# A two-layer hybrid decoder: the attention's values by seven block products, woven with queries, keys and memory keys, and fewer score steps

## The chip, the cores and the metric

The kernel runs on one core of a Trainium2 chip. A core has a matmul engine (PE, with its weight loads shown as PEld), a vector engine (DVE), a scalar engine (ACT), a general engine (POOL) and a queue engine (SP). Each runs its own instructions in order, and they wait for each other by semaphores. PE reads from the on-chip memory SBUF and writes to PSUM, which has eight banks of 128 x 512 floats. DMAs are issued from the queues of SP, ACT and POOL; only those issued from POOL can add to what they find at their destination.

The metric is the device time of one execution in microseconds (us), as the median of several runs. Everything is float32 at the input and the output.

## The reference

There are two decoder layers over 256 tokens of width 1024. Each layer is a half-step SwiGLU network, a token mixer, cross-attention into 256 memory tokens, and another half-step network. The change touches the mixer of layer 0, differential attention, and the memory keys of layer 0. Cut to what matters:

```python
def diff_attention(h, cos, sin, w_in, ..., subln, w_out, lambda_init):
    q, k, v = split(h @ w_in, 3)                 # 1024 columns each
    q = apply_rope(q, cos, sin) * (64 ** -0.5)   # 8 heads x 2 x 64; the factor is 0.125
    k = apply_rope(k, cos, sin)
    # v: 8 heads x 128
    s = einsum("bqhcd,bkhcd->bhcqk", q, k)       # two score matrices per head
    s = where(k_pos <= q_pos, s, -inf)
    p = softmax(s)
    a = p[:, :, 0] - lam * p[:, :, 1]
    o = einsum("bhqk,bkhe->bqhe", a, v)
    o = rmsnorm(o, subln) * (1.0 - lambda_init)
    return o @ w_out

def memory_cross_attention(h, mem, mem_norm, w_q, w_kv, w_o):
    k, v = split(rmsnorm(mem, mem_norm) @ w_kv, 2)   # 1024 columns each
    ...
```

## The kernel before

**Precision and granules.** Every large product is made of three matmuls (`mm3`, L262 to L264): each operand is split into a high part in the reduced format fp32r and a low part that is the rest, and high x high, high x low and low x high are summed in PSUM. A weight is loaded by SP into one of nine buffers of 1 MB (`wp`) and split in *granules* of 128 x 1024: ACT casts the high part (`whi`, L224), DVE subtracts for the low part (`wlo`, L225). Four buffers for each part (`hp`) limit how far the splits can run ahead of PE; the program asks for them two to three granules ahead (`ready`, `use`, `AHEAD`). A *host step* below is one granule used for both blocks of 128 tokens: twelve matmuls of 512 columns.

**Products.** `wide` multiplies all tokens by 512 columns: 8 row tiles x 2 token blocks x 3 = 48 matmuls. `stream` and `columns` make the same in steps that can be woven with others. `seven` makes a product of 2 x 2 blocks (token blocks x halves of the input width on one side, halves of the input width x two blocks of 512 columns on the other) from seven block products instead of eight. It needs sums of blocks: on the token side `combine` makes four (`mixes=True` in `Norm`; DVE sums, then ACT and DVE split them into `s_hi` and `s_lo`, L480 to L487), and on the weight side there are x1 = w11 + w12, x2 = x1 + w22, x4 = x2 + w21, x3 = w12 + w22. A weight sum (`Sum`, L187 and following) is made by DVE (L203) or by two accumulating DMAs of POOL (L199), each on one half of the tile. x2 and x4 are made in place on x1. A product step of `seven` takes one granule and makes six matmuls. Its products collect in two PSUM banks, and intermediate values are copied out in between. Both networks of each layer run `seven` for most gate and up columns; cross-attention runs it for its memory values.

**The order of work.** The builder keeps a planned clock (`Pipe`): each matmul group advances it, and follow-up work is registered with a due time (`pipe.after(us, f)`, the numbers in `T`), or with a due time and a condition (`pipe.when`). It is put into the program when the planned clock passes that time. Instructions then go to each engine in an order fixed when the kernel is built. `share` and `weave` interleave host steps with the fourteen product steps of a `seven`: the list of counts says how many host steps stand before each product.

**The attention stage** (`diff_attention`, about 189 to 313 us of the profile). Four `wide` calls make queries and keys of heads 0 to 3, then of heads 4 to 7. After each, `rope` rotates them (DVE, with an addition on POOL, L930), PE turns them (`qkt`, L939). After each key call four groups of `probs` follow, one for each head: ten short matmuls for two score matrices with their masks (`sc`, L970 to L974), then for both score matrices the maximum of each query block (L978, L979), the scaling by 0.125 (L980), the exponentials with their sums (ACT, L982, L984), the reciprocals, the factor lambda (L988), and the weighted difference (L990, L991). PE turns the result (`tp`, L997). Two `wide` calls make the values; `v_fin` scales them by the norm's factor (L1009). `heads` multiplies (`po`), normalises (`on`, L1030), turns (`otp`, L1035) and splits (`o_hi`, `o_lo`) for the output product. Between values and output stand half of the memory keys (`kv.k_units(kv.k_split, cs=(0,))`), which need the memory tokens fetched (`kv.fetch`, four DMAs on ACT's queue) and split (`kv.prep`, `mh` and `ml`). `out_b` is the output product in eight units of twelve matmuls; the input rows 4 to 7 of it are heads 4 to 7.

Of the kernel before, what the change touches and what calls it, by code (L numbers as in the profile page):

```python
# [15 lines left out]
P = 128  # L16
# [41 lines left out]
def trunk(ctx, tc, a, out):  # L58
# [302 lines left out]
    def seven(b1, b2, x, mix, after, order=(0, 1, 2, 3, 5, 4, 6), second="dma"):  # L361
# [3 lines left out]
        x1 = Sum(b11, b12)  # L365
# [60 lines left out]
    def out_b(src, nkt, lhs, fin, order, hooks={}):  # L426
# [18 lines left out]
        for half, k0 in [(c, k) for k in order for c in range(2)]:  # L445
            if (half, k0) in hooks:
                units.append(([], hooks[half, k0]))
            w = W(src, k0, 4, half * 512, 512)
            for k in range(k0, k0 + 4, 2):
                units.append(([Gran(k, 2, (w, 0, 512))], lambda *gr, half=half: run(*gr, half=half)))  # L450

# [447 lines left out]
    def diff_attention(norm, nxt, kv):  # L899
# [7 lines left out]
        def tables():  # L907
# [6 lines left out]
            tab["t"] = t  # L914

        def rope(ps, key):
# [4 lines left out]
            for t in range(2):  # L921
                c, s, n = (tab["t"][:, i + t, :] for i in (0, 2, 4))
# [10 lines left out]
            def turn():  # L933
# [9 lines left out]
                if key[0] == "k":  # L943
                    for i in range(4):
                        pipe.after(T["probs"][i], lambda i=i: probs(2 * key[1] + i // 2, i % 2))
            pipe.after(T["rot"], turn)

        def proj_fin(key):
            def fin(ps):
                if key == ("k", 1):  # L950
# [10 lines left out]
        def probs(c, j):  # L961
# [11 lines left out]
            for b in range(2):  # L973
                nc.tensor.matmul(sc[b].rearrange("p (i k) -> p i k", k=P)[:, 0:3:2, :], lhsT=id_bf, rhs=mask_bf,  # L974
                                 start=False, stop=True)
            for b in range(2):
                s = sc[b]
                nc.vector.tensor_reduce(st[:, 2 * b:2 * b + 1], s[:, 0:128], axis=AX.X, op=ALU.max, negate=True)  # L978
                nc.vector.tensor_reduce(st[:, 2 * b + 1:2 * b + 2], s[:, 128:384], axis=AX.X, op=ALU.max, negate=True)  # L979
                nc.vector.tensor_scalar(st[:, 4 + 2 * b:6 + 2 * b], st[:, 2 * b:2 * b + 2], 0.125, None, op0=ALU.mult)  # L980
                p = work("p", 384)
                nc.scalar.activation(p[:, 0:128], s[:, 0:128], AF.Exp, scale=0.125,  # L982
                                     bias=st[:, 4 + 2 * b:5 + 2 * b], accum_out=st[:, 8 + 2 * b:9 + 2 * b])
                nc.scalar.activation(p[:, 128:384], s[:, 128:384], AF.Exp, scale=0.125,  # L984
                                     bias=st[:, 5 + 2 * b:6 + 2 * b], accum_out=st[:, 9 + 2 * b:10 + 2 * b])
                ps.append(p)
            nc.vector.reciprocal(st[:, 12:16], st[:, 8:12])
            nc.vector.tensor_scalar(st[:, 14:16], st[:, 14:16], nlam, None, op0=ALU.mult)  # L988
            for qb, sl in ((0, slice(0, 128)), (1, slice(128, 384))):
                nc.vector.tensor_scalar(ps[0][:, sl], ps[0][:, sl], st[:, 12 + qb:13 + qb], None, op0=ALU.mult)  # L990
# [696 lines left out]
```

## Time and profile before

| | |
|---|---|
| median of 3 runs | 1257.79 us (1257.74 to 1258.11) |
| profiled execution, whole | 1258.38 us |
| its span, first to last instruction | 1256.6 us |
| granted PE clock | 0.999 |
| attention stage | about 189 to 313 us |
| weight DMAs of `da_w_in` from SP | 12 of 1 MB, median 5.2 us to land |
| accumulating DMAs of POOL | 72 of 512 KB |

The profile is of one execution. Its page gives, for each engine, the time in which it was busy; matmuls overlap in the pipeline, so that PE at 99% says that PE had always something under way, not that it ran at its peak. What PE costs is read from the distance between the starts of its matmuls. The list of waits says who stood still for whom. A wait that isn't in PE's list cost the kernel nothing, however long it was.

### The profile page before, as it was taken

How to read it: one execution, taken by the hardware profiler on the slowest of the kernel's cores; microseconds unless marked ns; L12 is line 12 of the kernel's file. 1: busy time of each engine (PE TensorE's matmuls, PEld its weight loads, DVE VectorE, ACT ScalarE, POOL GpSimd, SP SyncE). 2: the span in 40 equal slices, each digit the busy share in tenths (PEclk: the TensorE clock that was granted, in tenths of full speed). 3: DMA queues.
4: the chain of work that ended last, by engine and by line, in shares of the span. 5: the costliest groups of instructions: out<-in, count | busy, mean ns of one | idle time of the engine just before them, and what ended most of it. 6: DMA issues, size and time to landing. Idle time of an engine off the chain costs nothing.

```text
span 1256.6 us, 18186 instructions
## 1 busy us (share of the span) xinstructions
PE 1247.1 (99%) x6751; PEld 1071.7 (85%) x6751; DVE 1057.2 (84%) x1451; ACT 873.5 (70%) x1388; POOL 162.5 (13%) x139
## 2 busy tenths in 40 slices
PE   9999999999999999999999999999999999999997
PEld 7888888788998888888888889999998898888886
DVE  6998787887787999887998976798898887898886
ACT  6676764686676776767776756777876775877772
POOL 1101102101101111110111000022233100011100
PEclk9999999999999999999999999999999999999999
DMA  9989976445776688987879977665636586489961
GB/s 330 301 255 259 314 256 208 137 165 170 222 214 170 165 252 260 293 246 234 240 198 268 311 247 221 192 193 168 201 134 185 169 246 182 157 251 256 258 190 34
DMA packets 161195, 275.03 MB, mean 219 GB/s; under 512 B 7209, under 2 KB 43730, under 8 KB 161106
## 3 DMA queue, kind: packets, MB, share of 16 engines
q1 hardware_dynamic: 137744, 229.75, 53.4%
q0 software_dynamic: 19744, 38.28, 17.7%
q10 hardware_dynamic: 3618, 5.84, 1.4%
q8 instruction: 53, 0.87, 0.3%
q14 instruction: 36, 0.29, 0.1%
HBM read 271.72 MB, written 2.13 MB: 218 GB/s over the span
## 4 chain that ended last, share of the span: by engine, by line
PE 94%; DMA 2%; DVE 2%; ACT 2%; issue 1%; POOLq 0%; POOL 0%; SPq 0%; ACTq 0%; DVEq 0%
PE out L262 9%; PE out L264 9%; PE out L263 9%; PE seven L263 8%; PE seven L262 8%; PE seven L264 8%; PE htp L855 1%; PE up L263 1%; PE up L264 1%; PE up L262 1%; PE xs L264 1%; PE xs L262 1%; PE xq L263 1%; PE xq L264 1%; PE xs L263 1%; PE xq L262 1%
## 5 line engine op out<-in xcount | busy, mean ns | idle before, releaser
L225 DVE TENSOR_TENSOR wlo<-w,whi 128x1024 fp32r<-128x1024 f32 (+2 forms) x532 | 639.4, 1220 | 134.6 <-ACT whi L224 126.8
L224 ACT CAST whi<-w 128x1024 fp32r<-128x1024 f32 (+2 forms) x534 | 551.0, 1039 | 245.2 <-PE out L264 84.0
L262 PE MATMUL out<-whi,hid_hi 128*128 128x512 f32 x336 | 132.3, 394 | 0.0
L264 PE MATMUL out<-whi,hid_lo 128*128 128x512 f32 x336 | 131.0, 390 | 0.0
L263 PE MATMUL out<-wlo,hid_hi 128*128 128x512 f32 x336 | 130.8, 389 | 0.0
L263 PE MATMUL seven<-wlo,s_hi 128*128 128x512 f32 x272 | 106.0, 390 | 0.6 <-DVE wlo L225 0.6
L262 PE MATMUL seven<-whi,s_hi 128*128 128x512 f32 x272 | 106.2, 390 | 0.0
L264 PE MATMUL seven<-whi,s_lo 128*128 128x512 f32 x272 | 105.9, 389 | 0.0
L199 POOL DMA_DIRECT2D w<-in_ffn_w_up_dram x30 | 36.7, 1268 | 346.6 <-DVE wlo L225 339.5
L203 DVE TENSOR_TENSOR w<-w 128x2048 f32<-128x2048 f32 x32 | 73.2, 2287 | 2.0 <-DMA w<-in_ffn_w_gate_dram 1.5
L264 PEld LDWEIGHTS out<-whi,hid_lo 128*128 128x128 f32 x336 | 63.1, 188 | 13.4
L263 PEld LDWEIGHTS out<-wlo,hid_hi 128*128 128x128 f32 x336 | 63.1, 188 | 12.6
L262 PEld LDWEIGHTS out<-whi,hid_hi 128*128 128x128 f32 x336 | 63.1, 188 | 12.5
L262 PE MATMUL seven<-whi,xh 128*128 128x512 f32 x180 | 70.5, 392 | 0.0
L264 PE MATMUL seven<-whi,xl 128*128 128x512 f32 x180 | 70.1, 389 | 0.0
L263 PE MATMUL seven<-wlo,xh 128*128 128x512 f32 x180 | 70.0, 389 | 0.0
L263 PEld LDWEIGHTS seven<-wlo,s_hi 128*128 128x128 f32 x272 | 51.1, 188 | 11.4 <-DVE wlo L225 1.0
L264 PEld LDWEIGHTS seven<-whi,s_lo 128*128 128x128 f32 x272 | 51.1, 188 | 10.7
L262 PEld LDWEIGHTS seven<-whi,s_hi 128*128 128x128 f32 x272 | 51.1, 188 | 10.4
L199 POOL DMA_DIRECT2D w<-in_ffn_w_gate_dram x30 | 36.9, 1467 | 176.2 <-DVE xst L1146 62.3
L264 PEld LDWEIGHTS seven<-whi,xl 128*128 128x128 f32 x180 | 33.8, 188 | 7.1
L262 PEld LDWEIGHTS seven<-whi,xh 128*128 128x128 f32 x180 | 33.8, 188 | 6.8
(395 smaller groups left out, 3013.7 us busy)
## 6 DMA issues: line engine op xcount, KB each, us to landing
w<-in_ffn_w_up_dram SPq DMA_DIRECT2D x40, 1024.0 KB, 7.8
w<-in_ffn_w_down_dram SPq DMA_DIRECT2D x40, 1024.0 KB, 9.3
w<-in_ffn_w_gate_dram SPq DMA_DIRECT2D x38, 1024.0 KB, 8.9
w<-in_ssd_w_in_dram SPq DMA_DIRECT2D x24, 1024.0 KB, 5.4
w<-in_xa_w_kv_dram SPq DMA_DIRECT2D x16, 1024.0 KB, 6.4
w<-in_ffn_w_gate_dram POOLq DMA_DIRECT2D x30, 512.0 KB, 9.7
w<-in_ffn_w_up_dram POOLq DMA_DIRECT2D x30, 512.0 KB, 7.2
w<-in_da_w_in_dram SPq DMA_DIRECT2D x12, 1024.0 KB, 5.2
```

The costliest lines, as they stand in the source:

```text
L199: nc.gpsimd.dma_start(self.t[:, k:k + 2, :], w.src[r0:r0 + 2 * P, w.c0:w.c0 + w.n] .rearrange("(k p) c -> p k c", p=P), accum_op=ALU.add)
L203: nc.vector.tensor_tensor(self.t, self.l.t, w.t, op=ALU.add)
L224: nc.scalar.copy(hv, src)
L225: self.eng.tensor_tensor(self.lo[:, :, o:o + n], src, hv.bitcast(F32), op=ALU.subtract)
L262: nc.tensor.matmul(o, lhsT=lh, rhs=rh, start=start, stop=False, skip_group_check=onto)
L263: nc.tensor.matmul(o, lhsT=lh, rhs=rl, start=False, stop=False, skip_group_check=onto)
L264: nc.tensor.matmul(o, lhsT=ll, rhs=rh, start=False, stop=stop, skip_group_check=onto)
L855: nc.tensor.transpose(tp[:, j, t * P:(t + 1) * P], us[t][:, (i + j) * P:(i + j + 1) * P], ident)
```

## The change

It does five things, all in layer 0's attention.

1. The values come from one `seven` over both blocks of 512 columns (w11 from column 2560, w12 from column 2048) in place of two `wide` calls, with a new `v_fin` for the evictions. `Norm` for this stage now makes the token-side sums (`mixes=l == 0`). x1 is no longer a DVE sum of two loaded tiles: a new argument `first="dma"` loads a second copy of w11 and lets DMAs add w12 to it; x2 is added by DMA as well.
2. The fourteen product steps are woven with twenty host steps: queries and keys of heads 0 to 3, of heads 4 to 7, and the memory keys. The counts are 5, 3, 2, 2, 3, 2, 1; two host steps of memory keys are left for the end.
3. In `probs` one reduction of 384 columns gives three maxima (it was two reductions for each score matrix), and one tiny minimum joins the last two for both matrices. The factor 0.125 moves into a rotation table for the queries, and lambda goes into the second scalar of a scaling.
4. Due times: the second half's score groups come at 0.8 of their times, and their turning after 7.0 instead of 8.5.
5. `kv.fetch` and `kv.prep` come earlier, and the sixth and seventh of the eight output units change places, so that the rows of heads 6 and 7 are asked for last.

```diff
-    def seven(b1, b2, x, mix, after, order=(0, 1, 2, 3, 5, 4, 6), second="dma"):
+    def seven(b1, b2, x, mix, after, order=(0, 1, 2, 3, 5, 4, 6), second="dma", first=None):
...
-        x1 = Sum(b11, b12)
+        x1 = Sum(W(b1[0], 0, 4, b1[1], 512) if first else b11, b12, first)
         x2 = Sum(x1, b22, second)
...
+        if pairs:
+            units[-3], units[-2] = units[-2], units[-3]
...
-            tab["t"] = t
+            tq = slot("cossinq")[:, :192].rearrange("p (i f) -> p i f", f=32)
+            nc.vector.tensor_scalar(tq, t, 0.125, None, op0=ALU.mult)
+            tab.update(k=t, q=tq)
...
-                        pipe.after(T["probs"][i], lambda i=i: probs(2 * key[1] + i // 2, i % 2))
+                        pipe.after(T["probs"][i] * (0.8 if key[1] else 1.0), lambda i=i: probs(2 * key[1] + i // 2, i % 2))
...
-                if key == ("k", 1):
+                if key == ("k", 0):
                     kv.fetch()
...
+            top = st[:, 0:6].rearrange("p (b i) -> p b i", i=3)
             for b in range(2):
-                s = sc[b]
-                nc.vector.tensor_reduce(st[:, 2 * b:2 * b + 1], s[:, 0:128], axis=AX.X, op=ALU.max, negate=True)
-                nc.vector.tensor_reduce(st[:, 2 * b + 1:2 * b + 2], s[:, 128:384], axis=AX.X, op=ALU.max, negate=True)
-                nc.vector.tensor_scalar(st[:, 4 + 2 * b:6 + 2 * b], st[:, 2 * b:2 * b + 2], 0.125, None, op0=ALU.mult)
+                nc.vector.tensor_reduce(top[:, b, :], sc[b][:, 0:384].rearrange("p (i k) -> p i k", k=P), axis=AX.X,
+                                        op=ALU.max, negate=True)
+            nc.vector.tensor_tensor(top[:, :, 1], top[:, :, 1], top[:, :, 2], op=ALU.min)
+            for b in range(2):
                 p = work("p", 384)
-                nc.scalar.activation(p[:, 0:128], s[:, 0:128], AF.Exp, scale=0.125,
-                                     bias=st[:, 4 + 2 * b:5 + 2 * b], accum_out=st[:, 8 + 2 * b:9 + 2 * b])
-                nc.scalar.activation(p[:, 128:384], s[:, 128:384], AF.Exp, scale=0.125,
-                                     bias=st[:, 5 + 2 * b:6 + 2 * b], accum_out=st[:, 9 + 2 * b:10 + 2 * b])
+                for qb, sl in ((0, slice(0, 128)), (1, slice(128, 384))):
+                    o = 8 + 2 * b + qb
+                    nc.scalar.activation(p[:, sl], sc[b][:, sl], AF.Exp, bias=top[:, b, qb:qb + 1], accum_out=st[:, o:o + 1])
                 ps.append(p)
             nc.vector.reciprocal(st[:, 12:16], st[:, 8:12])
-            nc.vector.tensor_scalar(st[:, 14:16], st[:, 14:16], nlam, None, op0=ALU.mult)
...
-                nc.vector.tensor_scalar(ps[0][:, sl], ps[0][:, sl], st[:, 12 + qb:13 + qb], None, op0=ALU.mult)
-                nc.vector.scalar_tensor_tensor(ps[0][:, sl], ps[1][:, sl], st[:, 14 + qb:15 + qb], ps[0][:, sl],
+                nc.vector.tensor_scalar(ps[1][:, sl], ps[1][:, sl], st[:, 14 + qb:15 + qb], nlam, op0=ALU.mult, op1=ALU.mult)
+                nc.vector.scalar_tensor_tensor(ps[0][:, sl], ps[0][:, sl], st[:, 12 + qb:13 + qb], ps[1][:, sl],
                                                op0=ALU.mult, op1=ALU.add)
...
-            pipe.after(T["tp"], turn)
+            pipe.after(7.0 if c > 1 else T["tp"], turn)
...
+        def v_fin():
+            t, vs = {}, {}
+
+            def after(i, b):
+
+                def copy():
+                    t[i] = work(f"v{i}")
+                    nc.scalar.copy(t[i], b[i])
+
+                def put(r, n, x):
+                    vs[r, n] = slot("v")
+                    nc.scalar.activation(vs[r, n], x, AF.Copy, scale=norm.col[:, r:r + 1])
+                    if r:
+                        for c in (2 * n, 2 * n + 1):
+                            pipe.when(T["heads"] + 1.5 * (c - 2 * n), lambda c=c: {2 * c, 2 * c + 1} <= ats.keys(),
+                                      lambda c=c: heads(c, [vs[q, n] for q in range(2)]))
+
+                def c12():
+                    nc.vector.tensor_tensor(t[3], b[2], t[3], op=ALU.subtract)
+                    nc.scalar.copy(b[2], t[1])
+                    put(0, 0, t[3])
+
+                def c22():
+                    nc.vector.tensor_tensor(t[0], t[0], b[5], op=ALU.subtract)
+                    put(1, 0, t[0])
+                pipe.after(0.7, {0: copy, 1: copy, 3: copy, 2: c12, 5: c22, 4: lambda: put(0, 1, b[4]),
+                                 6: lambda: put(1, 1, b[6])}[i])
+                if i == 2:
                     kv.prep()
+            return after
...
-        for c in range(2):
-            wide([(w_in, c * 512, 512)], norm, "q", proj_fin(("q", c)))
-            wide([(w_in, 1024 + c * 512, 512)], norm, "k", proj_fin(("k", c)))
-        for c in range(2):
-            wide([(w_in, 2048 + c * 512, 512)], norm, "v", v_fin(2 * c))
-        kv.k_units(kv.k_split, cs=(0,))
-        out_b(a["da_w_out"][0], KT, ot, upd(1.0, nxt), (0, 4), {(0, 0): kv.fetch, (0, 4): kv.mix})
+            host += stream([(w_in, c * 512, 512)], norm, "q", proj_fin(("q", c)))
+            host += stream([(w_in, 1024 + c * 512, 512)], norm, "k", proj_fin(("k", c)))
+
+        def mk_fin(c):
+            def fin(ps):
+                kv.k[c] = ps
+                kv.k_split(c)
+            return fin
+        host += columns(a["xa_w_kv"][0], 0, kv, "mk", [mk_fin(0), mk_fin(1)])
+        weave(share(host, seven((w_in, 2560), (w_in, 2048), norm.x, norm.s, v_fin(), (1, 0, 3, 2, 5, 4, 6), "dma", "dma"),
+                    [5, 3, 2, 2, 3, 2, 1]))
+        out_b(a["da_w_out"][0], KT, ot, upd(1.0, nxt), (0, 4), {(0, 0): kv.fetch, (0, 4): kv.mix}, pairs=True)
...
-        nx = Norm(gains("mix_norm", l), first=l == 1)
+        nx = Norm(gains("mix_norm", l), first=l == 1, mixes=l == 0)
```

More of the change, by code (lines that the diff above doesn't have):

```diff
@@ L424, in down, with out_b @@
                 for k in range(w.k0, w.k0 + w.nk, 2)]
-    def out_b(src, nkt, lhs, fin, order, hooks={}):
+    def out_b(src, nkt, lhs, fin, order, hooks={}, pairs=False):
         banks = [[], []]
@@ L921, in rope @@
             for t in range(2):
-                c, s, n = (tab["t"][:, i + t, :] for i in (0, 2, 4))
+                c, s, n = (tab[key[0]][:, i + t, :] for i in (0, 2, 4))
                 x = ps[t].rearrange(r, x=2, f=32)
@@ L1000, in turn @@
                 ats[2 * c + j] = at
-            pipe.after(T["tp"], turn)
-        def v_fin(c0):
-            def fin(pv):
-                for c in range(c0, c0 + 2):
-                    v = v2(slot("v"))
-                    cs = slice((c - c0) * 256, (c - c0 + 1) * 256)
-                    for t in range(2):
-                        nc.scalar.activation(v[:, t, :], pv[t][:, cs], AF.Copy, scale=norm.col[:, t:t + 1])
-                    pipe.when(T["heads"] + 1.5 * (c - c0), lambda c=c: {2 * c, 2 * c + 1} <= ats.keys(), lambda c=c, v=v: heads(c, v))
-                if c0 == 0:
+            pipe.after(7.0 if c > 1 else T["tp"], turn)
[22 more added lines that the diff above has]
+                if i == 2:
                     kv.prep()
-            return fin
+            return after
         def heads(c, v):
@@ L1018, in heads @@
                 at = ats[2 * c + j]
-                vs = v[:, :, j * P:(j + 1) * P]
-                nc.tensor.matmul(po[:, j, 0, :], lhsT=at[:, 0:128], rhs=vs[:, 0, :], start=j == 0, stop=False)
-                nc.tensor.matmul(po[:, j, 1, :], lhsT=at[:, 128:256], rhs=vs[:, 0, :], start=False, stop=False)
-                nc.tensor.matmul(po[:, j, 1, :], lhsT=at[:, 256:384], rhs=vs[:, 1, :], start=False, stop=j == 1)
+                o = c % 2 * S + j * P
+                vs = [x[:, o:o + P] for x in v]
+                nc.tensor.matmul(po[:, j, 0, :], lhsT=at[:, 0:128], rhs=vs[0], start=j == 0, stop=False)
+                nc.tensor.matmul(po[:, j, 1, :], lhsT=at[:, 128:256], rhs=vs[0], start=False, stop=False)
+                nc.tensor.matmul(po[:, j, 1, :], lhsT=at[:, 256:384], rhs=vs[1], start=False, stop=j == 1)
             ss = sm.tile([P, 16], F32, name="ss", tag="ss")
@@ L1041, in heads @@
             pipe.after(T["otp"], turn)
+        host = []
         for c in range(2):
-            wide([(w_in, c * 512, 512)], norm, "q", proj_fin(("q", c)))
-            wide([(w_in, 1024 + c * 512, 512)], norm, "k", proj_fin(("k", c)))
-        for c in range(2):
-            wide([(w_in, 2048 + c * 512, 512)], norm, "v", v_fin(2 * c))
-        kv.k_units(kv.k_split, cs=(0,))
-        out_b(a["da_w_out"][0], KT, ot, upd(1.0, nxt), (0, 4), {(0, 0): kv.fetch, (0, 4): kv.mix})
+            host += stream([(w_in, c * 512, 512)], norm, "q", proj_fin(("q", c)))
[9 more added lines that the diff above has]
+        out_b(a["da_w_out"][0], KT, ot, upd(1.0, nxt), (0, 4), {(0, 0): kv.fetch, (0, 4): kv.mix}, pairs=True)
     def split2(src, name):
```

## The prediction

> **What bounds the kernel now.** I read the page's busy times and its chain of waits first, then the list of who waited for whom on the matmul engine.
>
> ```profile
> span 1256.6 us, 18186 instructions
> PE 1247.1 (99%) x6751; PEld 1071.7 (85%) x6751; DVE 1057.2 (84%) x1451; ACT 873.5 (70%) x1388; POOL 162.5 (13%) x139
> ...
> PE 94%; DMA 2%; DVE 2%; ACT 2%; issue 1%; POOLq 0%; POOL 0%; SPq 0%; ACTq 0%; DVEq 0%
> ```
> ```profile
> PE warm L597 <- DVE warm L99: 1.5, 1, 1.5
> PE seven L263 <- DVE wlo L225: 0.6, 1, 0.6
> PE acs L1285 <- PE mk L264: 0.2, 1, 0.2
> ```
>
> The chain that ended last is 94% PE, and the second fence is the whole list of PE's waits: 2.3 us in 1256.6, none of it in the attention stage. So the time is the number of matmuls times the pace at which they start. A matmul left out is paid in full; work added to another engine costs nothing until it makes PE wait, and then it is paid in full too.
>
> The next view gives busy times by stretch (us, then busy us of PE, PEld, DVE, ACT, POOL, then clock, DMA share, GB/s): the attention stage, its first half, the FFN that follows, and that FFN's densest 40 us.
>
> ```profile
> 190.00:313.00 123.00, 123.00 (x694) 102.08 (x694) 97.00 (x203) 80.16 (x195) 20.29 (x15) 1.00 0.52 171
> 190.00:256.00 66.00, 66.00 (x345) 52.49 (x344) 52.73 (x112) 37.31 (x81) 13.76 (x9) 1.00 0.54 187
> 410.00:540.00 130.00, 130.00 (x593) 107.92 (x593) 117.67 (x115) 94.60 (x111) 17.16 (x14) 1.00 0.83 238
> 420.00:460.00 40.00, 40.00 (x186) 33.27 (x185) 38.57 (x37) 29.50 (x36) 4.93 (x4) 1.00 0.79 227
> ```
>
> The clock is 1.00 throughout. DVE has 26.0 us free in the attention stage (123.00 less 97.00). The FFN, which already runs seven products for eight, keeps PE full with DVE busy for 90% of 130 us, and for 96% (38.57 of 40) in its densest part. That is the yardstick for what the stage will bear.
>
> **The matmuls.** The values are now two `wide` calls of 48 matmuls of 512 columns, 96 in all. `seven` makes 7 products x 4 k x 3 = 84. Twelve go. Their price stands in the FFN's timeline of PE, where one product starts exactly twelve matmuls after another:
>
> ```profile
> 441.08 0.39 PE L262 MATMUL seven<-whi,s_hi 128*128 128x512 f32 x1
> ...
> 443.80 0.39 PE L262 MATMUL seven<-whi,xh 128*128 128x512 f32 x1
> ```
>
> 443.80 - 441.08 = 2.72 us (0.227 each; the shown 0.39 overlaps its neighbours). Queries, keys, memory keys, scores, transposes and the output keep their number of matmuls: they only change places. **The whole gain is 2.72 us**, provided PE still never waits.
>
> **What DVE gets and loses.** Rows of the view that groups instructions by line and shape (xcount | busy us, mean ns of one | idle before):
>
> ```profile
> L225 DVE TENSOR_TENSOR wlo<-w,whi 128x1024 fp32r<-128x1024 f32 x36 | 45.6, 1278 | 13.2 <-ACT whi L224 13.2
> L979 DVE TENSOR_REDUCE st<-sc 128x1 f32<-128x256 f32 x16 | 6.6, 412 | 0.0
> L978 DVE TENSOR_REDUCE st<-sc 128x1 f32<-128x128 f32 x16 | 4.5, 279 | 2.4 <-PE sc L974 2.4
> L980 DVE TENSOR_SCALAR st<-st 128x2 f32<-128x2 f32 x16 | 2.5, 159 | 0.1
> L988 DVE TENSOR_SCALAR st<-st,lam 128x2 f32<-128x2 f32 x8 | 1.8, 223 | 0.1
> L459 DVE SCALAR_TENSOR_TENSOR ml<-my,cols,mh 128x256 fp32r<-128x256 f32 x8 | 3.5, 478 | 0.0
> ```
> ```profile
> L1140 DVE TENSOR_REDUCE xst<-xs 128x2 f32<-128x512 f32 x4 | 2.7, 682 | 0.0
> L486 DVE TENSOR_TENSOR s_lo<-sraw,s_hi 128x512 fp32r<-128x512 f32 x4 | 2.7, 683 | 0.0
> L837 DVE TENSOR_TENSOR p<-p,seven 128x512 f32<-128x512 f32 x4 | 2.7, 680 | 0.0
> L481 DVE TENSOR_TENSOR sraw<-y 128x256 f32<-128x256 f32 x4 | 1.5, 417 | 0.0
> ```
>
> - Seven products split 14 granules of weights where two `wide` calls split 8: 6 x 1.278 = +7.7.
> - `mixes=True`: eight block sums and four low parts, 8 x 0.417 + 4 x 0.683 = +6.1.
> - `c12` and `c22` (as L837): 2 x 0.68 = +1.4.
> - The scores lose 16 x (0.412 + 0.279 + 0.159) + 8 x 0.223 = 15.4 and get 16 reductions of 384 columns and eight tiny minima. The trace has no such reduction; it lies between 0.412 (256 columns) and 0.682 (512). I take the middle, 0.55: 8.8 + 8 x 0.16 = 10.1, net -5.3 (the ends of that bound: -7.5 to -3.2).
> - The query table, one instruction on 192 elements, lies between 0.16 (L980) and 0.417 (L481): taken as 0.3, near the smaller.
>
> Together +10.2: 107.2 of 120.3 us, 89%, under the FFN's 90%. On that average it is hidden. Uncovered it would cost what exceeds the room, which is the last rival.
>
> **ACT and POOL.**
>
> ```profile
> L224 ACT CAST whi<-w 128x1024 fp32r<-128x1024 f32 x91 | 95.4, 1052 | 38.7 <-PE out L264 16.2 <-PE seven L264 12.3 <-issue 2.7
> ...
> L547 ACT ACTIVATE y<-xt,cols 128x256 f32<-128x256 f32 x8 | 3.1, 480 | 0.0
> ...
> L833 ACT ACTIVATE p<-p,rcol 128x512 f32<-128x512 f32 x4 | 2.9, 721 | 0.0
> ```
>
> ACT gets 6 splits (6.3), 8 copies of y (3.8), and 12 instructions on 512 columns (four high parts, four copies, four value evictions) at 0.72 or less (8.7): 80.2 + 18.8 = 99.0 of 120.3 at most, before the eight old value evictions are taken off. Not a bound. SP's queue issues one more weight load (the second copy of w11); the DMA share of 0.52 leaves room.
>
> POOL gets the eight issues of four sums; L199's issues run 1.2 to 1.74 us:
>
> ```profile
> L199 POOL DMA_DIRECT2D w<-in_ffn_w_gate_dram x30: 1197/1533/1742, 48.8 to 1173.7; - x30
> ...
> DMA to landing us min/median/max: 5.7/7.4/13.8
> ```
>
> Three of the four sums have several products' time to land. **The tight one is x2**, built in place on x1 with only two host steps between the product that reads x1 and the one that reads x2. Cross-attention does this same chain now; POOL's and PE's timelines show its lead:
>
> ```profile
> 325.58 1.23 POOL L199 DMA_DIRECT2D w<-in_xa_w_kv_dram  x1 [5.45 <-DVE xsq L1127]
> 328.39 1.22 POOL L199 DMA_DIRECT2D w<-in_xa_w_kv_dram  x1 [1.58 <-DVE wlo L225]
> ```
> ```profile
> 331.19 0.40 PE L262 MATMUL seven<-whi,s_hi 128*128 128x512 f32 x1
> ```
>
> The halves of x2 go out 5.6 and 2.8 us before x1's product starts (331.19), as x1's granules are split. At the median 7.4 they land at +1.8 and +4.6. PE asks for x2 at +2.72 (the product) + 5.44 (two host steps of twelve matmuls) = +8.2 and, for the second half, at +9.5; whi and wlo take 1.05 + 1.28 of that. So 4.0 and 2.6 us are to spare: I cost it at nothing. Both at the longest landing, 13.8, would be 2.4 and 3.8 late. Behind a sum that waits on POOL stand the first keys' rotation additions and the next sums; behind x2's `wlo` on DVE stand the first score groups; and PE waits for both.
>
> The Trainium skill's page "DMA: Bandwidth & Descriptors", section "Anatomy of one DMA", puts such a transfer at 2 us plus its bytes at 436 GB/s, an estimate of 3.2 us for 512 KB. The quickest here took 5.7, so I go by the trace; by the page the sum would be the same with more to spare.
>
> **What moves.** The memory keys' 96 matmuls go ahead of the output, with `prep` and the fetch of the memory blocks (four DMA issues of ACT) ahead of them; the work is the same, and the same DMAs stood in ACT's queue before. `seven` holds two of the eight PSUM banks through the whole stage, which the old values did not: a score group that finds no free bank would wait, in the same place and for the same time as in the first rival below, where I count it. I cost the moves at nothing.
>
> **The end of the stage.** Fewer score steps shorten the chain maxima, exponentials, scaling, transposes, heads, output. But the planner now allows 7.0 us for the last four groups where it allowed 8.5, and the values end later relative to the output. The last group of before, by line (PE's and DVE's timelines):
>
> ```profile
> 265.48 0.49 PE L970 MATMUL sc<-qk 64*128 64x128 f32 x4
> ...
> 278.54 0.49 PE L997 MATMUL tp<-ident,p 128*128 128x128 f32 x3
> ```
> ```profile
> 276.38 0.74 DVE L991 SCALAR_TENSOR_TENSOR p<-p,st 128x128 f32<-128x128 f32 x2
> ```
>
> Its p was done at 277.12, 1.4 us before PE transposed it. Allowing 1.5 less while the group saves some 0.7 of DVE time (5.3 / 8) leaves about +0.6. I cost it at nothing, with little cover; the bounds are 0 and 1.5 us for each of four groups, and a first wait also lets DVE catch up, so that I count two of the four at most (3.0).
>
> **The sum.** 1256.6 - 2.72 = 1253.9 for the profiled span. The profiled execution took 1258.38, 1.8 more than its span, and lies 0.6 above the median of the timed runs, so on that median: 1257.79 - 2.72 = **1255.1 us**, 0.22% less. About 0.2% (2.5 us) is what a measurement of this kernel can tell from no change, so a wait of only 0.2 us already turns it from faster to the same.
>
> **The rivals.**
>
> *A late group of scores (0.25).* The 1.4 us of spare above speak for it, PE's empty list of waits against. One wait of 1.5: 1256.6; range 1255.4 to 1258.1.
>
> *x2 lands late (0.10).* With the longest landing, up to 3.8: 1258.9. Against it stands a DMA share of 0.52 here.
>
> *DVE becomes the bound between the first query step and the last key step, and the kernel is slower (0.13).* Sixteen host steps and ten product steps stand there now. PE's own time for them:
>
> ```profile
> 189.38 0.39 PE L262 MATMUL q<-whi,xh 128*128 128x512 f32 x1
> ```
> ```profile
> 242.09 0.39 PE L262 MATMUL v<-whi,xh 128*128 128x512 f32 x1
> ```
>
> From 189.38 to 242.09 sixteen host steps with their transposes and scores took 52.7; ten product steps of 1.36 make 66.3. DVE's row for 190 to 256 was 52.73. Into the same time come about 6.5 more granules (8.3), the mixes (6.1), c12 and c22 (1.4) and the memory's low parts (8 x 0.478 = 3.8), less four score groups' saving (2.6): 69.7, or 3.4 over, unless the fourth rotation and fifth score group, which fall after this point in the new order, take their share out again (the rotation is 2.6 by the two rows below, the group about as much: an estimate of 5): 64.7, 1.6 under.
>
> ```profile
> 243.35 0.68 DVE L925 TENSOR_TENSOR rt<-k,cossinr 128x512 f32<-128x512 f32 x1
> ...
> 245.54 0.41 DVE L929 TENSOR_TENSOR rt<-k,cossinr 128x256 f32<-128x256 f32 x1
> ```
>
> It decides against the change when DVE's need there passes 66.3 + 2.7 = 69.0. POOL could push it there: beside the rotation's addition on POOL a split took 2.00 us for 1.22,
>
> ```profile
> 202.73 2.00 DVE L225 TENSOR_TENSOR wlo<-w,whi 128x1024 fp32r<-128x1024 f32 x1
> ```
>
> and eight new POOL issues at 0.78 each are 6.2: 64.7 + 6.2 = 70.9, 4.6 over, 1259.7; with the 5 staying in, 1264.7. I give this rival the middle, 1262. The Trainium skill's page "SBUF — State Buffer", section "SBUF: two separate sides", says that a DVE instruction with two SBUF inputs and a GpSimd one that reads SBUF hold the shared ports as an exclusive lock; the 2.00 agrees. Against this rival: in the FFN's densest 40 us four such issues (4.93 us of POOL) ran with DVE at 96% and PE never waited.
>
> That the change doesn't do what it says is no rival for the matmuls, which are counted in the code; for the score steps it is: they lie off the chain, so their 5.3 us of DVE buy no time by themselves.
>
> **Chances.** Forecast, no wait over 0.3 us: 0.52, of it 0.46 faster by over 0.2%. With the rivals: faster 0.46, the same 0.43 (small waits and most of the first two rivals), slower 0.11. The likeliest case's own range is 1254.6 to 1255.4; the 8-in-10 range reaches through the first two rivals, 1254.6 to 1258.9.
>
> **What would show it.** Right: 12 fewer matmuls, PE's list of waits still about 2.3 us, DVE near 107 of some 120 us in the stage. First rival: PE waiting for p at L997's place, or for `on` or `o_lo`. Second: `wlo` of x2 waiting for a DMA, and PE behind it. Third: whi done early, wlo late, PE waiting for wlo in many places, splits beside POOL well over 1.22.

## The result and the profile after

The changed kernel takes 1265.61 us (median of 6 runs, 1264.07 to 1266.41), the kernel before 1257.93 (6 runs, 1257.74 to 1258.33) beside it. The ratio is 1.0059, with a 95% interval of 1.0046 to 1.0072: slower, where 1255.1 was forecast with a range up to 1258.9. The profiled execution took 1265.59, its span 1263.8. Lines of the changed file are shifted: score matmuls are L974 to L978, the rotation's addition L934, the copy of the turned queries and keys (`qk`) L945, the copy of the turned scores (`at`) L1002.

From the page after, the line of busy times and the one of the chain; then the four largest entries of the list of who PE waited for (total us, times, longest):

```profile
PE 1248.7 (99%) x6739; PEld 1071.4 (85%) x6739; DVE 1069.4 (85%) x1440; ACT 886.3 (70%) x1406; POOL 174.8 (14%) x147
...
PE 78%; DVE 2%; issue 0%; ACT 0%; POOL 0%; POOLq 0%
```
```profile
PE sc L974 <- ACT qk L945: 2.6, 1, 2.6
PE po L1043 <- ACT at L1002: 2.1, 2, 1.2
PE warm L599 <- DVE warm L99: 1.5, 1, 1.5
PE qkt L943 <- POOL rt L934: 0.9, 1, 0.9
```

Twelve matmuls fewer, as counted (6739 for 6751), and yet PE is busy 1.6 us longer. Three of the four are new, and all stand in attention. PE's timeline gives the stage's first matmul and the first one behind it, then the first one behind it in the kernel before:

```profile
189.06 0.39 PE L262 MATMUL q<-whi,xh 128*128 128x512 f32 x1
```
```profile
320.45 0.28 PE L262 MATMUL mk<-mh,whi 128*128 128x256 f32 x1
```
```profile
313.06 0.28 PE L262 MATMUL mk<-mh,whi 128*128 128x256 f32 x1
```

320.45 - 189.06 = 131.39 us; before it was 313.06 - 189.38 = 123.68. The difference, 7.71, is the whole loss (1265.61 - 1257.93 = 7.68). With the 2.72 that went, PE lost 10.4 us inside the stage. The windows (PE, PEld, DVE, ACT, POOL, granted clock, DMA share, GB/s) say where, and that waits are not all of it; the last row is the kernel before:

```profile
190.00:256.00 66.00, 62.41 (x306) 49.35 (x305) 57.71 (x106) 43.79 (x89) 13.66 (x11) 0.97 0.71 203
190.00:320.00 130.00, 124.31 (x679) 101.76 (x678) 109.49 (x189) 90.80 (x208) 25.70 (x19) 0.97 0.65 192
...
190.00:223.00 33.00, 32.12 (x152) 26.50 (x151) 31.55 (x50) 20.57 (x32) 8.71 (x8) 1.00 0.82 235
...
227.50:231.00 3.50, 3.47 (x14) 2.46 (x15) 2.13 (x4) 0.92 (x3) 1.20 (x1) 0.53 1.09 201
...
293.50:296.00 2.50, 2.50 (x9) 2.06 (x9) 2.50 (x5) 1.48 (x9) 0.43 (x1) 0.58 0.28 61
```
```profile
190.00:223.00 33.00, 33.00 (x164) 27.12 (x164) 23.35 (x38) 16.12 (x23) 7.65 (x5) 1.00 0.57 194
```

On the average of the stage DVE is at 109.49 of 130 us, 84%. In its first 33 us it is at 31.55, 96%, for 23.35 before. And right behind the long waits the clock is granted at 0.53 and 0.58. What that costs is seen by run 1 below, where the same matmuls run with the clock at 1.00: from the first score matmul behind the wait to the next product it is 3.26 us here (227.53 to 230.79) and 1.78 there, and from the `po` at 292.46 to the next transpose 3.64 here and 2.16 there. That is about 1.5 us each. With the waits (2.6 + 2.1 + 0.9) it makes 8.6 of the 10.4; for the rest the list has no entry over 0.2 in the stage.

**The largest wait, backwards.** ACT's timeline, then POOL's, DVE's and PE's:

```profile
225.00 1.99 ACT L224 CAST whi<-w 128x1024 fp32r<-128x1024 f32 x2 [4.35 <-DMA w<-in_da_w_in_dram]
226.90 1.06 ACT L945 COPY qk<-qkt 128x512 f32<-128x512 f32 x2
```
```profile
209.64 1.24 POOL L199 DMA_DIRECT2D w<-in_da_w_in_dram  x1 [14.59 <-DVE cossinr L915]
211.22 2.96 POOL L934 TENSOR_TENSOR rt<-rt,rt 128x512 f32<-128x512 f32 x2 [0.34 <-DVE rt L933]
215.86 1.20 POOL L199 DMA_DIRECT2D w<-in_da_w_in_dram  x1 [1.68 <-ACT qk L945]
```
```profile
212.98 3.42 DVE L225 TENSOR_TENSOR wlo<-w,whi 128x1024 fp32r<-128x1024 f32 x2
```
```profile
216.43 0.39 PE L262 MATMUL seven<-whi,s_hi 128*128 128x512 f32 x1
...
227.53 0.80 PE L974 MATMUL sc<-qk 64*128 64x128 f32 x4 [2.55 <-ACT qk L945]
```

Read upwards from PE: the first score matmul (227.53) waits for `qk`, which ACT has copied late because the split of x2's second half stands ahead of it in ACT's queue, and that stood 4.35 us for its DMA. The DMA went out at 215.86, after DVE had split x1's second granule. That split, the first of the two in DVE's row, took 2.29 us for 1.22, behind the rotation and beside POOL's additions. (POOL's row names ACT's `qk` as the last event ahead of the issue; in run 9 the row of the same issue names the split.) x1's product starts at 216.43, so the second half had 0.6 us of lead, and it landed after 9.0 us (the view of DMA issues, for that one).

### The profile page after: what moved, and what is told of

It is laid out like the page before. It is cut to its first block, busy times and chain, and to the rows that moved or that the text cites. A ratio compares the mean times of both kernels' runs of the same rounds, so it can differ in the third digit from the quotient of the medians.

```text
span 1263.8 us, 18179 instructions
## 1 busy us (share of the span) xinstructions
PE 1248.7 (99%) x6739; PEld 1071.4 (85%) x6739; DVE 1069.4 (85%) x1440; ACT 886.3 (70%) x1406; POOL 174.8 (14%) x147
## 4 chain that ended last, share of the span: by engine, by line
PE 78%; DVE 2%; issue 0%; ACT 0%; POOL 0%; POOLq 0%
PE out L262 7%; PE out L264 7%; PE out L263 7%; PE seven L263 7%; PE seven L262 7%; PE seven L264 7%; PE xs L264 2%; PE xs L262 2%; PE xs L263 2%; PE xq L263 1%; PE xq L264 1%; PE xq L262 1%; PE htp L857 1%; PE py L1484 1%; PE z L262 1%; PE z L264 1%
## 5 line engine op out<-in xcount | busy, mean ns | idle before, releaser
L225 DVE TENSOR_TENSOR wlo<-w,whi 128x1024 fp32r<-128x1024 f32 (+2 forms) x538 | 647.6, 1222 | 129.8 <-ACT whi L224 122.0
L224 ACT CAST whi<-w 128x1024 fp32r<-128x1024 f32 (+2 forms) x540 | 556.8, 1040 | 239.2 <-PE out L264 82.9
L263 PE MATMUL seven<-wlo,s_hi 128*128 128x512 f32 x288 | 112.3, 390 | 0.6 <-DVE wlo L225 0.6
L262 PE MATMUL seven<-whi,s_hi 128*128 128x512 f32 x288 | 112.6, 391 | 0.0
L264 PE MATMUL seven<-whi,s_lo 128*128 128x512 f32 x288 | 112.2, 389 | 0.0
L262 PE MATMUL seven<-whi,xh 128*128 128x512 f32 x192 | 75.6, 394 | 0.0
L264 PE MATMUL seven<-whi,xl 128*128 128x512 f32 x192 | 74.8, 390 | 0.0
L263 PE MATMUL seven<-wlo,xh 128*128 128x512 f32 x192 | 74.7, 389 | 0.0
L263 PEld LDWEIGHTS seven<-wlo,s_hi 128*128 128x128 f32 x288 | 54.1, 188 | 12.4 <-DVE wlo L225 1.4
L262 PEld LDWEIGHTS seven<-whi,s_hi 128*128 128x128 f32 x288 | 54.2, 188 | 11.1
```

The costliest lines, as they stand in the source:

```text
L224: nc.scalar.copy(hv, src)
L225: self.eng.tensor_tensor(self.lo[:, :, o:o + n], src, hv.bitcast(F32), op=ALU.subtract)
L262: nc.tensor.matmul(o, lhsT=lh, rhs=rh, start=start, stop=False, skip_group_check=onto)
L263: nc.tensor.matmul(o, lhsT=lh, rhs=rl, start=False, stop=False, skip_group_check=onto)
L264: nc.tensor.matmul(o, lhsT=ll, rhs=rh, start=False, stop=stop, skip_group_check=onto)
```

## The experiments

Theory A: the three waits are separate; the largest is x2's DMA on ACT's queue. Theory B: DVE is the bound, and the waits only show where its lateness surfaces. Others joined as runs ruled them in. Each ratio is to the kernel before.

**1. x2 by DVE.**

```diff
-v_fin(), (1, 0, 3, 2, 5, 4, 6), "dma", "dma")
+v_fin(), (1, 0, 3, 2, 5, 4, 6), "dve", "dma")
```

> The changed kernel, but x2 = x1 + w22 is made by DVE (one addition of 128x2048, 2.29 us in the changed kernel's profile) and not by two accumulating DMAs. Theory A (the time is lost at three single places; the largest is x2's second half, which lands at about 224.9 us and holds ACT's queue, the first keys' qk copies and the score matmuls behind it: 2.7 us of gap and about 2 us of matmuls at half pace): the gap at 224.6 goes and the time falls by 4 to 5 us, to 1260.5 to 1261.6. Theory B (DVE is the bound of the stage, the waits only show where its lateness surfaces): DVE gets 2.3 us more work in its densest stretch, and the time stays or grows, 1265.6 to 1268.

1262.41, ratio 1.0033 (1.0020 to 1.0046): 3.2 us less, with 2.3 us more work on DVE, and 0.8 over A's range. The profiled execution lost 1.7 us in the kernel's first 6 us, where PE waited for a DMA of constants (L603), far from the edit. Its attention stage, measured as above, takes 127.25 us, 4.1 less than the 131.39 of the changed kernel. The gap and the low clock behind it are gone. But PE now waits twice for the rotation:

```profile
PE po L1043 <- ACT at L1002: 2.1, 2, 1.2
PE qkt L943 <- POOL rt L934: 2.0, 2, 1.2
```

So A's wait was real, and B has a part: the rotation stands behind a full DVE (31.91 of the first 33 us).

**2. x2 asked for one host step later.**

```diff
-[5, 3, 2, 2, 3, 2, 1]
+[5, 3, 3, 1, 3, 2, 1]
```

> The changed kernel, but one more host step (twelve matmuls, 2.72 us) stands between x1's product and x2's, and one less between x2's and the next. No work is added or taken. Theory A: x2's second half has 2.7 us more to land, the gap at 224.6 and the half pace behind it go, 1261 to 1262. Theory B: the same work for DVE, so the gap turns up elsewhere in the stretch, 1264.5 to 1266.

The wait for `qk` stayed, 2.3 us in the trace: the second half went out at 216.47 and landed after 9.8, and the split still stood ahead of the `qk` copies in ACT's queue. The median is 1262.22 (1.0040, 1.0025 to 1.0055), but the profiled run took 1265.3 and its trace doesn't explain the other three at about 1262. Inconclusive on the time. On the mechanism A's forecast that the gap goes fails: this one trace speaks for the place in ACT's queue as what matters, and not for the moment at which PE needs x2.

**3 and 4. The end of the stage: head products later, and the old due times.**

```diff
-lambda c=c: heads(c, [vs[q, n] for q in range(2)]))
+lambda c=c: pipe.after(3.0 if c == 2 else 0.0, lambda: heads(c, [vs[q, n] for q in range(2)])))
```

> The changed kernel, but the first head product of the second half (heads 4 and 5) comes 3.0 us later in the planned order, so that output matmuls stand ahead of it while ACT's copies of the turned scores are made. Theory A: the two gaps at 289.1 and 291.0 (1.06 and 1.37) and the half pace behind them (0.95) go, 3.4 us: 1262.2 (1261.5 to 1263). Theory B: the whole chain of scores is late, PE then waits for the heads' normalising or splitting (otp, o_lo) instead: 1264.5 to 1265.6.

```diff
-pipe.after(T["probs"][i] * (0.8 if key[1] else 1.0), ...
+pipe.after(T["probs"][i], ...
-pipe.after(7.0 if c > 1 else T["tp"], turn)
+pipe.after(T["tp"], turn)
```

> The changed kernel with the due times of before: the second half's score groups at their full times, and their turning planned 8.5 us after the scores for 7.0. Theory A (the copies at are late because they stand in ACT's queue behind the next group's exponentials, which wait for DVE): the transposes only move later in PE's order, no gain, 1264.5 to 1266.5. Rival C (the shortened due times of the change made the wait at po): the 3.4 us at 289 to 295 go, 1262.2.

1264.17 (1.0048, 1.0031 to 1.0065) and 1263.91 (1.0048, 1.0033 to 1.0063): 1.4 and 1.7 less, half of what was at stake and between the theories' forecasts. In both, the waits at `po` went and others came. The list of PE's waits, of the first and of the second:

```profile
PE out L264 <- DVE o_lo L461: 1.6, 1, 1.6
```
```profile
PE otp L1058 <- DVE on L1053: 1.2, 1, 1.2
...
PE out L264 <- DVE o_lo L461: 0.7, 1, 0.7
```

So far the chain of the last heads looks late as a whole, and the old due times only move its wait (1.9 us for 2.1). Run 11 tests its order.

**5, 6 and 7. Keys or all hosts earlier, and the rotation's additions on DVE**, all on top of run 1.

```diff
-[5, 3, 2, 2, 3, 2, 1]
+[5, 4, 4, 3, 1, 1, 1]      (k1_early)
+[8, 4, 3, 1, 1, 1, 1]      (values_later)
-nc.gpsimd.tensor_tensor(t1, t1, t2, op=ALU.add)
+nc.vector.tensor_tensor(t1, t1, t2, op=ALU.add)      (rot_on_dve)
```

> x2_by_dve (1262.4) with the counts 5, 4, 4, 3, 1, 1, 1: the second keys' last host step stands behind three products and not five, 5.4 us earlier, and the last products and the memory keys are left to fill the time of the last score groups. Theory E (the end waits because the last four score groups start late: their keys' last matmul is at 262.6 us and PE runs out of memory keys at 289): the two gaps at po (2.4) and the half pace behind them (about 1) go, 1259 (1258.5 to 1259.7). Theory B (DVE and ACT haven't the room for these groups beside the splits of three more products): PE waits as long elsewhere, 1261.5 to 1264.

> x2_by_dve (1262.4) with the counts 8, 4, 3, 1, 1, 1, 1: eight host steps ahead of the first product for five. Theory D (DVE is full from 196 to 223 us, where the token sums, the tables, the first rotations and two products' splits come together, so that the first queries' rotation is late and qkt waits twice, 2.15): a host step asks one split of DVE for 2.72 us of PE, a product two, so DVE gets room, the two waits go, and the last keys come earlier as in k1_early: 1257 to 1258. Theory B: the products bunch up later and DVE is short there: 1260 to 1263.

> x2_by_dve (1262.4) with the rotation's additions on DVE in place of POOL, eight of 128x512. Theory P (POOL's additions are what is late: 1.3 to 2.25 us each, and they slow a split beside them from 1.22 to about 2.29): DVE pays 8 x 0.68 = 5.4 us and gets back about 6 x 1.07 = 6.4, qkt no longer waits for POOL: 1260.4 to 1261.4. Theory D: DVE has more to do where it is full, 1262.4 to 1264.

k1_early 1263.75 (1.0046, 1.0031 to 1.0061) and values_later 1264.78 (1.0056, 1.0041 to 1.0071): worse than run 1's 1262.41, so E fails and D's cure too. The waits moved: in k1_early 3.2 us for POOL's rotation in three places, in values_later 3.2 for `o_lo`. rot_on_dve 1260.1 (1.0019, 1.0009 to 1.0028): 2.3 better, with 5.4 us *more* work on DVE. Its two waits for the rotation are gone, and one of 1.1 for a split of the second keys is new. That speaks for P, and against a plain count of DVE's work.

**8. Nothing but the score steps, on the kernel before.** The edit is part 3 of the change, its core:

```diff
+nc.vector.tensor_reduce(top[:, b, :], sc[b][:, 0:384].rearrange("p (i k) -> p i k", k=P), axis=AX.X,
+                        op=ALU.max, negate=True)
...
+nc.vector.tensor_tensor(top[:, :, 1], top[:, :, 1], top[:, :, 2], op=ALU.min)
```

> The kernel before with nothing but the changed score steps (one reduction of 384 columns for two, one minimum, 0.125 in a query table, lambda in the scaling). DVE saves 5 us in the stage, PE's matmuls are the same. All theories in which PE's list of waits sets the time: no difference, 1257.9 (within 0.3). A rival in which the time follows DVE's work: 1255 to 1257.

1259.0 (1.0008, 0.9999 to 1.0018). DVE's reductions of 384 columns took 0.549 each. No gain, and the rival falls. But the time is 1.1 over the forecast, outside its 0.3, though the interval of the ratio includes 1. In its trace PE waits 1.1 us longer for constants at the kernel's start, far from the edit, and the stage itself is 0.5 us longer (124.19 for 123.67).

**9 and 10. The additions alone, and DVE without the token sums**, both on the changed kernel with x2 by DMA.

```diff
-nc.gpsimd.tensor_tensor(t1, t1, t2, op=ALU.add)
+nc.vector.tensor_tensor(t1, t1, t2, op=ALU.add)      (rot_alone)
...
-combine(self.y, self.s, [5.0 + 1.6 * i for i in range(8)])
+for i, w in enumerate((6.6, 11.4, 13.0, 16.2)):      (no_sums)
+    pipe.after(w, lambda i=i: cut(i))    # cut: hi = copy of y[i]; s[i] = (hi, hi)
```

> The changed kernel (1265.6) with only the rotation's additions on DVE; x2 is still summed by DMA. Theory P (POOL's additions, which slow the splits of x1 beside them from 1.22 to about 2.3, are why x2's second half goes out late): the gap at 224.6 goes too, 1260 to 1261. Theory D (DVE is full there in any case: two additions of 0.68 take what the slow splits gave back): x2's second half goes out within 1 us of the same time, the score matmuls still wait over 1.5 for the qk copy, 1262 to 1264.

> The changed kernel without the token-side sums: the four products that read sums read plain tokens, in high and low part alike, so that DVE loses eight block sums and four low parts (6.1 us) between 194 and 214 us; ACT's copies, the weights' sums by DMA, the matmuls and POOL's additions stay. Theory D (DVE, full from 194 to 223, is the root of the late rotation and of x2's late issue): x2's second half goes out 3 us or more sooner, qkt and score matmuls wait under 0.5 there, 1259.5 to 1261 with the end's waits left. Theory A alone (the DMA's 9 us of landing and its place ahead of the qk copies in ACT's queue): the issue hangs on x1's product, the gap stays over 1.5, 1263.5 to 1265.

rot_alone 1259.49 (1.0016, 1.0007 to 1.0026): this one line takes back 6.1 of the 7.7 us. POOL's and DVE's timelines of it:

```profile
214.22 1.20 POOL L199 DMA_DIRECT2D w<-in_da_w_in_dram  x1 [3.54 <-DVE wlo L225]
```
```profile
212.64 1.22 DVE L225 TENSOR_TENSOR wlo<-w,whi 128x1024 fp32r<-128x1024 f32 x1
...
214.98 2.35 DVE L225 TENSOR_TENSOR wlo<-w,whi 128x1024 fp32r<-128x1024 f32 x2
```

x2's second half goes out 1.6 us sooner and lands after 6.0 for 9.0, so that it is there 4.6 us earlier, the larger part of it by the quicker landing. Nothing waits there, although DVE is as full (windows of rot_alone, then of no_sums):

```profile
190.00:223.00 33.00, 33.00 (x156) 27.39 (x155) 32.29 (x55) 22.47 (x34) 4.20 (x4) 1.00 0.87 249
```
```profile
190.00:223.00 33.00, 33.00 (x158) 27.47 (x157) 27.33 (x40) 21.19 (x34) 10.87 (x8) 1.00 0.90 252
```

no_sums 1260.71 (1.0024, 1.0015 to 1.0034): 4.9 less, with POOL's additions where they were. Its second half went out at 212.99 and landed after 9.6; the wait for `qk` is 0.4. So either lightening DVE by 6.1 us or taking POOL's additions out of the chain is enough to clear this wait. D was right that room on DVE cures it, wrong that nothing else does: its forecast for rot_alone fails.

**11 and 12. The same on rot_on_dve: the end's order, and the earlier keys.**

```diff
-pipe.after(7.0 if c > 1 else T["tp"], turn)
+pipe.after((6.0, 7.0)[c - 2] if c > 1 else T["tp"], turn)      (rot_tail)
-lambda c=c: heads(c, [vs[q, n] for q in range(2)]))
+lambda c=c: pipe.after(1.5 if c == 2 else 0.0, lambda: heads(c, [vs[q, n] for q in range(2)])))      (rot_tail)
-[5, 3, 2, 2, 3, 2, 1]
+[5, 4, 4, 3, 1, 1, 1]      (rot_k1_early)
```

> rot_on_dve (1260.1) with an earlier turning of heads 4 and 5 (6.0 planned for 7.0), so that their copies stand ahead of the next groups' exponentials in ACT's queue, and their head product 1.5 us later. Theory F (the end's wait is a matter of order in ACT's queue: in the changed kernel p of heads 4 was done at 280.0, its transposes came at 285.74 and its copy at 289.79): the waits at po (2.15) go and nothing of over 0.5 takes their place, 1258 (1257.4 to 1258.7). Theory B (the whole chain is late): waits for on or o_lo, 1259.5 to 1260.5.

> rot_on_dve (1260.1) with the counts of k1_early (5, 4, 4, 3, 1, 1, 1). In k1_early PE waited 3.2 for POOL's additions in the bunched stretch and 1.3 for o_lo at the end. Theory P: the former go, 1259 to 1260 (o_lo's waits stay). Theory B: DVE with the additions and with three products' splits beside the last score groups is short, 1261 to 1263.

1258.8 (1.0007, 0.9998 to 1.0017) and 1262.74 (1.0044, 1.0027 to 1.0061). The first is 1.3 less and 0.1 over F's range: `po` waits no more, B's waits for `on` or `o_lo` don't come, and one wait of 1.0 for p is left. In the changed kernel p of heads 4 was done by 280.0 and its copy `at` stood in ACT's queue until 289.79, behind the exponentials of the next groups; turning it earlier puts the copy ahead of them. The earlier keys lose in this form too, as B has it.

**13 and 14. Is it POOL's work or its place?** rot_echo is rot_alone plus eight additions on POOL for nobody; PE, DVE and ACT run rot_alone's instructions in the same order. before_rot is the kernel before with the additions on DVE.

```diff
+nc.gpsimd.tensor_tensor(t2, t2, t2, op=ALU.add)
```

> rot_alone (1259.5) with POOL's eight additions put back beside it, on data that nobody reads any more, so that nothing waits for them; PE's, DVE's and ACT's instructions are those of rot_alone in the same order. Theory G (POOL's work itself costs: a split beside it takes 2.0 to 2.3 for 1.22, and an accumulating DMA in flight lands 2 to 3 us later): most of the loss comes back, 1262 to 1265. Theory H (the additions cost by standing in the chain from the rotation to the transposes and by the order that follows from it): 1259 to 1260.5.

> The kernel before with only the rotation's additions on DVE. Its PE waits for nothing in the stage and DVE has 26 us free there. All theories: no difference, 1257.8 (within 0.6). If it were faster by 1 or more, rot_alone's gain would have little to do with the change.

rot_echo 1263.2 (1.0047, 1.0032 to 1.0062): 3.7 of the 6.1 come back. before_rot 1257.88 (1.0001, 0.9991 to 1.0010): nothing. PE's waits in rot_echo, and DVE's and POOL's timelines:

```profile
PE k L263 <- DVE wlo L225: 2.5, 1, 2.5
PE po L1044 <- ACT at L1003: 2.1, 2, 1.2
```
```profile
215.72 3.74 DVE L225 TENSOR_TENSOR wlo<-w,whi 128x1024 fp32r<-128x1024 f32 x2
...
248.39 3.63 DVE L461 SCALAR_TENSOR_TENSOR ml<-my,cols,mh 128x256 fp32r<-128x256 f32 x7
```
```profile
215.73 1.50 POOL L935 TENSOR_TENSOR rt<-rt 128x512 f32<-128x512 f32 x1
```

POOL's work beside DVE costs by itself: two splits that took 2.35 in rot_alone take 3.74, POOL's addition of 1.50 in the midst of them. But not at the place where the changed kernel lost: there is no wait for `qk`, the wait is 1.0 in rot_alone and 2.5 here, for a split at 250 us, and in this execution the clock falls behind it. So G holds for the cost, but not for the landings: x2's halves landed after 6.0 and 6.6. The wait at x2 did not come back with POOL's work alone, which speaks for H there. It is not shown: DVE's order in rot_echo is that of rot_alone, with x1's split ahead of a token sum's low part (`s_lo`) that stands ahead of it in the changed kernel.

**15 to 18. What is left.** dma_tail is rot_alone with rot_tail's later `po` and the due times below; dma_tail_counts adds the counts.

```diff
-pipe.after(7.0 if c > 1 else T["tp"], turn)
+pipe.after((6.0, 8.5)[c - 2] if c > 1 else T["tp"], turn)      (dma_tail)
-[5, 3, 2, 2, 3, 2, 1]
+[5, 3, 2, 3, 3, 1, 1]      (dma_tail_counts)
```

> rot_alone (1259.5) with heads 4 and 5 turned 6.0 after their scores and their head product 1.5 later, as in rot_tail, and heads 6 and 7 turned after 8.5 for 7.0, since rot_tail's PE waited 1.0 there for p. Theory F (the end is a matter of order): both the waits at po (2.2) and the one for p stay away, 1257 to 1258. Theory B: a wait of 1 us or more for on or o_lo, 1258.5 to 1259.5.

> dma_tail with the counts 5, 3, 2, 3, 3, 1, 1: one more host step ahead of the fourth product, two fewer before the sixth. Theory I (PE's wait of 1.0 for wlo at 250 us in rot_alone is DVE's shortage where four score groups and the fourth and fifth product's splits meet): it shrinks to under 0.4 and the last keys come one product earlier, 1256 to 1257. Theory B: DVE is short a few us later, no gain over dma_tail or a loss.

1258.69 (1.0008, 0.9998 to 1.0017) and 1259.63 (1.0016, 1.0006 to 1.0025). Both are as B has it: `po` waits no more, but `o_lo` takes 1.1, and the counts don't cure the wait at 250 us, they move it (1.3 for `wlo` of the memory keys). DVE's timeline of dma_tail shows what stands ahead of that split:

```profile
247.01 2.85 DVE L461 SCALAR_TENSOR_TENSOR ml<-my,cols,mh 128x256 fp32r<-128x256 f32 x7
249.78 1.22 DVE L225 TENSOR_TENSOR wlo<-w,whi 128x1024 fp32r<-128x1024 f32 x1
```

The memory's low parts, in one block. prep_spread sets its four pairs apart; prep_tail then turns heads 4 and 5 after 5.5 and asks for their `po` 0.5 later.

```diff
-for p in range(KT // 2):
-    ...
+for p in range(KT // 2):
+    pipe.after(2.0 * p, lambda p=p: pair(p))
```

> dma_tail (1258.7) with the four pairs of the memory's splits 2.0 us apart in the planned order for all at once. Theory J (PE's wait at 250 us is the burst of eight ml ahead of the keys' wlo on DVE, moved work that was costed at nothing): the wait of 1.0 goes, 1257.3 to 1257.8. Theory I (DVE is short there on average, whatever its order): the wait turns up at the next split, 1258.4 to 1259.

> prep_spread with heads 4 and 5 turned after 5.5 for 6.0 and their head product 0.5 later for 1.5, so that their normalising starts 1 us sooner. Theory F: the wait for o_lo (1.1 in dma_tail) halves or goes, 1256.5 to 1257.3, under the kernel before (1257.8). Theory B: PE waits for the transposes or at po instead, no gain over prep_spread.

1257.89 (1.0000, 0.9992 to 1.0009) and 1256.85 (0.9995, 0.9986 to 1.0004; 11 runs, 9 of them from 1256.68 to 1256.99, two at 1258.29 and 1258.88). J (0.1 over its range) and F hold. The list of PE's waits in prep_tail, apart from those outside the stage:

```profile
PE tp L1000 <- DVE o_lo L461: 0.3, 1, 0.3
```

With its waits cleared the change beats the changed kernel by 8.8 us. Over the kernel before its median is 1.0 lower, and the interval of the ratio includes 1: a gain was not shown. Of the 2.72 forecast 1.7 are missing. The stage takes 122.89 us for 123.67 before, so they are missing inside it; 0.3 is the wait above, for the rest PE's list has no wait in the stage, and it stays open.

## Why the prediction was wrong

- **The matmuls.** "The whole gain is 2.72 us", "provided PE still never waits": the count was right, the condition was not met. The error is in the places below, which the forecast each costed at nothing. That a matmul left out is paid in full was not shown either: with PE's waits cleared but for 0.3 us (prep_tail) the stage is 0.8 us shorter.
- **x2, the step that failed most.** "So 4.0 and 2.6 us are to spare: I cost it at nothing." The lead was taken from cross-attention (5.6 and 2.8 us ahead of x1's product), where no rotation and no token sums stand on DVE. Here it was 6.8 (216.43 - 209.64) and 0.6, and the landings 8.3 and 9.0. The need was mis-set too: it was taken from x2's own product, while ACT takes its split earlier and has the `qk` copies behind it. I named who stands behind x2 on POOL and on DVE, and not on ACT, where PE's wait came from. The rival priced up to 3.8; the wait was 2.6, and the low clock behind it cost another 1.5.
- **DVE.** The sum held: 109.49 in 130 us, for 107.2 forecast; the reduction took 0.547 for 0.55, the query table 0.26 for 0.3. "On that average it is hidden" was the error: its work falls into the first 33 us, where it rose from 23.35 to 31.55 (the token sums, the splits, the rotation), and there it delays x1's splits. The third rival looked at 66 us and at a mean; its sign, waits for `wlo` in many places, never showed, since the lateness was handed on to POOL's DMA and to ACT. DVE's share of busy time was no measure either: rot_alone had 32.29 there and no wait.
- **POOL's additions** were in the forecast as a slow split beside them (2.00 for 1.22) within the third rival. The Trainium skill's page "SBUF — State Buffer", section "SBUF: two separate sides", has such a pair as an exclusive lock; rot_echo agrees (3.74 for 2.35 beside an addition of 1.50). What I missed is that they run beside the split in the chain to x2. One line that moved them was worth 6.1 us here and nothing in the kernel before.
- **"I cost the moves at nothing."** In the changed kernel no wait shows for them. Once the additions had moved, the memory's splits cost 0.8 (prep_spread), as a burst of DVE ahead of a split of the second keys.
- **The end.** The first rival had a wait of the last heads' chain, for p, `on` or `o_lo` (1.5, in 0.25). It came one step behind p, as 2.1 at `po`, for a copy that stood in ACT's queue behind the exponentials, plus 1.5 of low clock.
- **The score steps** buy no time by themselves: right (scores_only).
- **The cases were not exclusive.** The first two rivals came true together, with the front of the third. A list of what had been costed at nothing, each with the same engine behind it, was not several chances of which at most one falls due.

Open: why x2's second half landed after 9.0 to 9.8 us in the five kernels with x2 by DMA and the additions on POOL (the changed one, x2_one_later, po_later, old_dues, no_sums), and after 6.0 to 7.4 in the six with the additions on DVE (rot_alone, rot_echo, dma_tail, dma_tail_counts, prep_spread, prep_tail). The first half doesn't sort so: 5.8 to 8.3 and 5.9 to 8.3. POOL's work beside the DMA doesn't decide it alone, as rot_echo shows (6.6, beside an addition of 1.50); the fetch of the memory blocks goes out at about the same time in the changed kernel and in rot_alone, and no run set it apart. Moving the additions also changed the order in which DVE's and PE's instructions are put, so rot_alone doesn't separate the chain from the order.

## What to carry to other kernels

Read slack at the densest stretch of the engine that feeds PE, not over the stage: 84% on the average hid 96% in the first quarter. Even that only says where to look: rot_alone was at 98% there, and PE waited for nothing. For each transfer that may be late, list what stands behind its reader on every engine's queue, ACT's evictions above all, and set the need by the first of those. And a wait of PE can cost more than its length: the one of 2.55 us cost another 1.5 here.

## What the runs showed of the hardware

**A wait can lower the clock behind it, and need not.** In the traces single waits of PE of 2.28 us (x2_one_later), 2.47 (rot_echo), 2.55 (the changed kernel), 2.64 (old_dues) and 3.09 (po_later) were each followed by a stretch of the clock at 0.50. It was 3.4 us long, and 6.8 in po_later. (A window that takes in some of the full speed at its edges shows 0.53 or 0.58.) After the waits of 2.14 in values_later and rot_k1_early, and after the shorter ones that stood alone, it stayed at 1.00. The two waits at `po`, 0.9 and 1.2 within 3 us, were followed by a low stretch in the changed kernel and in rot_echo, and by none in x2_by_dve and no_sums: for such a pair these traces give no rule. Executions of one kernel differ in it too: the profiled one of rot_echo took 1265.24 at a mean clock of 0.997, its other three 1262.63 to 1263.63 at 0.999. Windows behind the wait of 3.09 in po_later, behind one of 1.18 in x2_by_dve, and around the wait of 1.21 at `po` in rot_alone:

```profile
228.50:235.00 6.50, 6.29 (x21) 4.67 (x22) 3.87 (x7) 3.58 (x12) 1.20 (x1) 0.53 0.78 129
```
```profile
225.50:228.00 2.50, 2.50 (x15) 1.94 (x14) 2.50 (x3) 1.18 (x2) 1.27 (x2) 1.00 0.87 307
```
```profile
287.00:290.00 3.00, 2.02 (x12) 1.80 (x13) 2.96 (x8) 3.00 (x14) 0.00 (x0) 1.00 0.53 203
```

The Trainium skill's page "TensorE: Matmul & The Clock Gate", section "What's actually happening", has the clock halved after an idle window of about 3.4 us, and full again after about as long of work. The half and the length agree with these rows; the idle time that it took here was shorter: 2.28 us for a single wait, and 0.90 and 1.21 together in the changed kernel.
